# Hybrid decoder block with experts: the residual's gate moves from the weights to the product, and the row writes change buffer and queue

## The chip, the cores and the metric

One core of one Trainium2 chip runs the whole program. The metric is device time in microseconds (us) of one execution.

## The reference, cut to what matters

512 tokens of width 1024 go through one block: a modulated norm, a mixer (causal convolution and gated linear attention), a gated residual, a second norm with a router, and 32 experts of which each token uses two.

```
mod = c_act @ w_ada[l] + b_ada[l]
sh1, sc1, ga1, sh2, sc2, ga2 = jnp.split(mod, N_MOD, axis=-1)
u = modulate(rmsnorm(h, g_norm1[l]), sh1, sc1)
y = hybrid_mixer(...)                    # ends with: merged @ w_out
h = h + ga1[:, None, :] * y
u2 = modulate(rmsnorm(h, g_norm2[l]), sh2, sc2)
y2 = hierarchical_moe(u2, ...)           # 32 experts: (silu(t@w1)*(t@w3))@w2
h = h + ga2[:, None, :] * y2
```

`ga1` has one value per output column, so `ga1 * (merged @ w_out)` can be had by scaling the columns of `w_out` or by scaling the product.

## The kernel before

**Engines and queues.** TensorE (PE) works in the order of the program text. VectorE (DVE), ScalarE (ACT) and GpSimd (POOL) get an order from a planner that goes by estimated times, except where a stretch is marked as ordered by hand. SyncE (SP) issues nearly all loads, strictly in the order of the text: a transfer whose buffer or data is not ready holds up everything behind it. A transfer can also be issued from ACT's instruction stream; it then stands in ACT's order.

**Mixer.** Each weight piece is loaded, cast by ACT into a high part (`hi`), and the rest (`lo`) is taken by DVE or POOL in turn (`low_part`, line 384); PE multiplies three passes of high and low parts (line 393). The last part of the mixer is eight tiles of `w_gla_o` (`fmgo`, from `rawgo`, `higo`, `logo`). Beside it run the sums over `w_ada` for the second norm, the gates and the final norm (`acc_...`).

**Output projection.** `load_wo(c, k4)` brings `w_out` for column half `c` into `wo0` and `wo1` (two buffers each): load `woraw`, multiply by the gate row `ga1r` on DVE, cast on ACT, rest on POOL or DVE. Half 0 is loaded during the mixer from ACT's queue, half 1 later from SP. Half 0 is multiplied for all four token tiles first; then the list `ORDER` sets by hand what PE, DVE and ACT do. A step is a letter, a token tile t and a half or a depth index: W is three passes of half 1 for one of eight k, E the residual (`hx` += product), T four transposes of `hx` and ACT's copy of them, L and F the router's logits, Q squares, N the norm's root, R the choice of experts, P the positions, S `split_row`, G the first gather of tokens by matmuls with a selection (`gxf`).

**split_row(t)** scales row tile t twice on ACT for each half, into `mhi` and into `scaled`; POOL takes `mlo` from both; then the 128 finished rows go from `scaled` to the DRAM tensor `rowsd`, from where later gathers fetch tokens. `scaled` has two buffers in one allocation. `ga1r` and `scaled` use one slot of the pool in turn (tag "rows"), which the experts' input `xt` takes next.

**Experts.** Weights come in half slabs of 1 MB. `half_slab` hands out 14 slabs, then the two buffers each of `wo0` and `wo1`, in a fixed ring. Thirteen half slabs are issued before the output projection ends. The next five need the buffers of `wo0` and `wo1` and the slab `spare` (which holds the router's weights), and stand on SP behind the four `rowsd` writes. All later ones need a slab that the experts' own matmuls set free. `layer` (L1352: `hag`, `hbg`) multiplies with w1 and w3, `outputs` (L1382: `pog`) with w2, in groups of two pairs of experts.

Of the kernel before, what the change touches and what calls it, by code (L numbers as in the profile page):

```python
# [14 lines left out]
ALU = mybir.AluOpType  # L15
PSUM = bass.MemoryType.PSUM

P = 128
S = 512
D = 1024  # L20
ND = D // P
# [39 lines left out]
def kernel(ctx: ExitStack, tc: tile.TileContext, a, dbg=None):  # L61
    nc = tc.nc
    V, A, G, T, SY = nc.vector, nc.scalar, nc.gpsimd, nc.tensor, nc.sync

    def tt(out, in0, in1, op):
        return V.tensor_tensor(out, in0, in1, op=op)  # L66
# [27 lines left out]
    def tl(tag, name, shape=None, dt=F32):  # L94
        n, w = LOW.get(tag) or HIGH[tag]
        return (plo if tag in LOW else pa).tile([P, w] if shape is None else list(shape), dt, tag=tag, bufs=n, name=name)
# [285 lines left out]
    def low_part(lo, raw, hi):  # L382
        turn[0] += 1
        (V if turn[0] % LO_EVERY < lo_v[0] else G).tensor_tensor(lo, raw, hi.bitcast(F32), op=ALU.subtract)  # L384
# [135 lines left out]
    for t in range(NT):  # L520
        pz = bank("g", f"pz{t}")
        us = slice(t * P, (t + 1) * P)
# [220 lines left out]
    def big(tag, name, shape, dt=F32):  # L743
        return pr.tile(list(shape), dt, tag=tag, bufs=SLOTS[tag], name=name)
# [3 lines left out]
    def late(tag, name, n=1, shape=(P, 512), dt=F32):  # L748
        return plate[0].tile(list(shape), dt, tag=tag, bufs=n, name=name)

    ga1r = big("rows", "ga1r", (P, D))

    w_o = a["w_out"][0].rearrange("(k p) f -> p k f", p=P)
    wo = {}
# [1 line left out]
    def load_wo(c, k4):  # L756
        if c:
            rows = pslab.tile([P, 4, 512], F32, tag="slab", bufs=NW, name=f"woraw{k4}")
            SY.dma_start(rows, w_o[:, 4 * k4:4 * k4 + 4, 512:D])
        for i in range(2):  # L760
            k = 4 * k4 + 2 * i
            if c:
                raw = rows[:, 2 * i:2 * i + 2]
            else:
                raw = tl("raw", f"woraw{c}{k}", (P, 2, 512))
                A.dma_start(raw, w_o[:, k:k + 2, 0:512])

            tt(raw, raw, ga1r[:, c * 512:(c + 1) * 512].unsqueeze(1).to_broadcast([P, 2, 512]), ALU.mult)
            w = big(f"wo{i}", f"wo{c}{k4}{i}", (P, 2, 2, 512), F32R)
            A.copy(w[:, 0], raw)  # L770
            low_part(w[:, 1], raw, w[:, 0])
            for e in range(2):
                wo[c, k + e] = w[:, 0, e], w[:, 1, e]
# [77 lines left out]
    background += ada_col([(bfc, cols5[:, 0:8], None, PLAIN)], 0, "bf", w_af)  # L851
    background += ada_col([(afc, cols5[:, 8:16], cols5[:, 16:24], PLAIN)], D, "af", w_af)
    background += [lambda k4=k4: load_wo(0, k4) for k4 in range(2)]


# [65 lines left out]
    rowsd = pd.tile([S, D], F32, name="rowsd")  # L921
# [67 lines left out]
    for k4 in range(2):  # L989
        load_wo(1, k4)  # L990
# [31 lines left out]
    half_logits, banks, outs = {}, {}, {}  # L1022
# [28 lines left out]

    def residual(t, c):
        cs = slice(c * 512, (c + 1) * 512)
        tt(hx[:, t, cs], hx[:, t, cs], outs[t, c], ALU.add)

    def squares(t, c):
# [50 lines left out]
    def split_row(t):  # L1107

        us = slice(t * P, (t + 1) * P)
        for c in range(2):  # L1110
            row = hx[:, t, c * 512:(c + 1) * 512].rearrange("p (i k) -> p k i", k=ND)
            half = slice(us.start + c * 64, us.start + c * 64 + 64)
            hi = mhi[:, :, half]
            A.activation(hi, row, AF.Copy, scale=r2[:, t:t + 1])
            lo = mlo[:, :, half]
            u = scaled[:, t % 2, :, c * 64:c * 64 + 64]
            A.activation(u, row, AF.Copy, scale=r2[:, t:t + 1])
            G.tensor_tensor(lo, u, hi.bitcast(F32), op=ALU.subtract)
        SY.dma_start(rowsd[us], scaled[:, t % 2].rearrange("p k i -> p (k i)"))

    def token_weights(t, last):

# [44 lines left out]
    def gather_first(t, kk):  # L1167
        if t == 0:
            gathered.append(bank("mm" if kk else "bg", f"gxf{kk}"))
        gather(gathered[kk], kk, t, sel0)  # L1170

    STEPS = {"W": part, "T": turned, "L": logits_half, "F": logits, "N": rms, "R": route, "P": positions,
             "S": split_row, "G": gather_first, "E": residual, "Q": squares}

    ORDER = """E00 E10 E20 E30 T00 W00 W01 T10 L00 W02 W03 T20 L10 W04 W05 Q00 T30 L20 W06 W07 Q10 L30 Q20 Q30
               E01 W10 W11 T01 Q01 W12 L01 N0 S0 W13 F0 R0 W14 W15 W16 W17
               E11 W20 W21 T11 P0 Q11 W22 L11 N1 S1 W23 F1 R1 W24 W25 W26 W27
               E21 W30 W31 T21 P1 Q21 W32 L21 N2 S2 W33 F2 R2 W34 W35 W36 W37
               E31 P2 G00 G01 T31 Q31 G02 G03 L31 N3 G10 S3 F3 G11 R3 G12 G13 G20 G21 P3 G22 G23 G30 G31 G32 G33"""
    scaled = big("rows", "scaled", (P, 2, ND, P))  # L1180
    V.memset(lgs, -BIG)
    iota0 = late("iota0", "iota0", 1, (P, NE), U32)
    V.tensor_scalar(iota0, slotno[:, 0:NE], -1.0, None, op0=ALU.add)
# [8 lines left out]
    with tc.manual_schedule(engines={mybir.EngineType.PE, mybir.EngineType.DVE, mybir.EngineType.Activation}):  # L1192
        for step in ORDER.split():
            STEPS[step[0]](*map(int, step[1:]))
# [107 lines left out]
    def experts(n, cols, wts, name, early=False, tail=False):  # L1302
# [113 lines left out]
        def ending(behind):  # L1416
# [11 lines left out]
            def join(x, t):  # L1428
                combine([1], *sums[x], t)
                norm(t, "ABC".index(x), *sums[x], V if (x, t) in (('A', 3), ('C', 1), ('C', 3)) else G)  # L1430
# [3 lines left out]
            STEPS.update({x: lambda t, x=x: join(x, t) for x in sums})  # L1434
            ORDER = """M00 H00 L00 M01 H01 L01 M02 H02 J00 J01 L02 J02 J03 M03 H03 L03 J10 J11 J12 J13 X
                       M10 H10 L10 M11 H11 L11 M12 H12 M13 L12 H13 A0 A1 L13 M14 H14 A2 A3 L14 M15 H15
                       B0 B1 L15 B2 B3 S1 C0 R0 C1 R1 W0 C2 R2 W1 C3 R3 W2 W3"""
            with tc.manual_schedule(engines={mybir.EngineType.DVE, mybir.EngineType.Activation}):
                for step in ORDER.split():
                    STEPS[step[0]](*map(int, step[1:]))  # L1440
# [87 lines left out]
```

## Time and profile before

| | |
|---|---|
| median of 3 runs | 1016.86 us (1016.12 to 1017.1) |
| the profiled execution's own time | 1016.93 us |
| its span, first to last instruction | 1015.2 us |
| mean granted TensorE clock | 0.985 |
| busy: PE, DVE, ACT, POOL | 943.9, 555.7, 341.5, 184.0 us |
| moved by DMA | 283.96 MB |

Busy time is an average over stages with different limits: a busy PE can be a PE that is fed just in time, and an engine with a low share can hold up all others for some microseconds. The stages have to be read one by one, by windows and by who waited for whom.

### The profile page before, as it was taken

How to read it: one execution, taken by the hardware profiler on the slowest of the kernel's cores; microseconds unless marked ns; L12 is line 12 of the kernel's file. 1: busy time of each engine (PE TensorE's matmuls, PEld its weight loads, DVE VectorE, ACT ScalarE, POOL GpSimd, SP SyncE). 2: the span in 40 equal slices, each digit the busy share in tenths (PEclk: the TensorE clock that was granted, in tenths of full speed). 3: DMA queues.
4: the chain of work that ended last, by engine and by line, in shares of the span. 5: the costliest groups of instructions: out<-in, count | busy, mean ns of one | idle time of the engine just before them, and what ended most of it. 6: DMA issues, size and time to landing. Idle time of an engine off the chain costs nothing. (4 is left out here: it accounts for less than half of the span.)

```text
span 1015.2 us, 13708 instructions
## 1 busy us (share of the span) xinstructions
PE 943.9 (93%) x5250; PEld 609.8 (60%) x5250; DVE 555.7 (55%) x1041; ACT 341.5 (34%) x694; POOL 184.0 (18%) x122
## 2 busy tenths in 40 slices
PE   7999999999899999899999998989999898999993
PEld 4778899888678887687753353533435343343442
DVE  6778899889875898964541232331322233121346
ACT  7657323474135554342861102011110201002214
POOL 5513434323231212311210000000000000000005
PEclk9999999999999999999999999999999999999997
DMA  9863233215843677639569999999999999999972
GB/s 283 234 162 84 84 91 98 84 45 185 268 148 82 210 231 265 207 105 416 233 264 422 421 421 422 420 421 421 419 423 420 421 421 420 421 419 422 363 232 86
DMA packets 122409, 283.96 MB, mean 280 GB/s; under 512 B 10819, under 2 KB 87339, under 8 KB 99044
## 3 DMA queue, kind: packets, MB, share of 16 engines
q1 hardware_dynamic: 112700, 252.21, 65.9%
q10 hardware_dynamic: 7624, 27.27, 7.8%
q0 software_dynamic: 2016, 3.56, 0.9%
q8 instruction: 43, 0.70, 0.3%
q14 instruction: 26, 0.21, 0.1%
HBM read 282.61 MB, written 4.19 MB: 282 GB/s over the span
## 5 line engine op out<-in xcount | busy, mean ns | idle before, releaser
L384 POOL TENSOR_TENSOR low<-raww,hiw 128x1024 fp32r<-128x1024 f32 x36 | 91.7, 2546 | 211.1 <-ACT hiw L410 210.2
L1382 PE MATMUL pog<-p_w,htg 128*64 128x512 f32 x448 | 107.5, 602 | 5.0 <-DMA p_w<-in_w 5.0
L1387 ACT CAST ohlg<-pog 128x512 fp32r<-128x512 f32 (+2 forms) x38 | 19.7, 518 | 259.7 <-DVE pog L69 259.7
L66 DVE TENSOR_TENSOR s1g<-s1g,hbg 128x512 f32<-128x512 f32 (+1 forms) x18 | 11.1, 628 | 167.0 <-PE hbg L1352 167.0
L69 DVE SCALAR_TENSOR_TENSOR conv<-z,cols,conv 128x511 f32<-128x511 f32 (+14 forms) x120 | 88.7, 739 | 5.5 <-ACT conv L482 1.8
L393 PE MATMUL fmw<-uhi,low 128*128 128x512 f32 x224 | 91.4, 408 | 0.0
L393 PE MATMUL fmw<-uhi,hiw 128*128 128x512 f32 x224 | 90.2, 403 | 0.7 <-ACT sg L490 0.3
L393 PE MATMUL fmw<-ulo,hiw 128*128 128x512 f32 x224 | 90.5, 404 | 0.0
L66 DVE TENSOR_TENSOR hx<-hx,pcg 128x512 f32<-128x512 f32 (+1 forms) x76 | 49.2, 658 | 66.5 <-PE pcg L1407 66.5
L1382 PEld LDWEIGHTS pog<-p_w,htg 128*64 128x64 f32 x448 | 34.0, 138 | 76.1 <-issue 63.5
L393 PE MATMUL tm<-low,uhi 128*128 128x256 f32 x256 | 72.2, 284 | 0.0
L393 PE MATMUL tm<-hiw,uhi 128*128 128x256 f32 x256 | 71.9, 285 | 0.0
L393 PE MATMUL tm<-hiw,ulo 128*128 128x256 f32 x256 | 71.6, 281 | 0.0
L410 ACT CAST hiw<-raww 128x1024 fp32r<-128x1024 f32 x44 | 46.0, 1046 | 75.9 <-issue 43.0
L69 DVE SCALAR_TENSOR_TENSOR pog<-pog,wslg,ga2r 128x512 f32<-128x512 f32 (+2 forms) x38 | 25.6, 674 | 78.2 <-PE pog L1382 78.2
L393 PEld LDWEIGHTS fmw<-uhi,hiw 128*128 128x128 f32 x224 | 42.7, 191 | 10.5 <-ACT sg L490 0.8
L393 PEld LDWEIGHTS fmw<-ulo,hiw 128*128 128x128 f32 x224 | 42.7, 191 | 10.0
L393 PEld LDWEIGHTS tm<-low,uhi 128*128 128x128 f32 x256 | 48.1, 188 | 0.9 <-issue 0.5
L393 PEld LDWEIGHTS fmw<-uhi,low 128*128 128x128 f32 x224 | 42.6, 190 | 9.8 <-DVE low L384 0.2
L393 PEld LDWEIGHTS tm<-hiw,uhi 128*128 128x128 f32 x256 | 47.7, 188 | 0.8 <-issue 0.5
L393 PEld LDWEIGHTS tm<-hiw,ulo 128*128 128x128 f32 x256 | 48.1, 188 | 0.1
L1358 ACT ACTIVATE s1g<-hag 128x512 f32<-128x512 f32 x16 | 9.6, 598 | 103.4 <-PE hag L1352 103.4
(476 smaller groups left out, 1878.6 us busy)
## 6 DMA issues: line engine op xcount, KB each, us to landing
p_w<-in_w SPq DMA_DIRECT2D x182, 1024.0 KB, 19.8
raww<-in_w_in SPq DMA_DIRECT2D x44, 512.0 KB, 4.0
adaw<-in_w_ada SPq DMA_DIRECT2D x32, 256.0 KB, 5.6
aw_ga<-in_w_ada ACTq DMA_DIRECT2D x8, 1024.0 KB, 5.3
p_w2part<-in_w SPq DMA_DIRECT2D x12, 512.0 KB, 15.6
aw_a<-in_w_ada ACTq DMA_DIRECT2D x4, 1024.0 KB, 7.2
aw_b<-in_w_ada ACTq DMA_DIRECT2D x4, 1024.0 KB, 5.1
aw_bf<-in_w_ada_f ACTq DMA_DIRECT2D x4, 1024.0 KB, 5.5
```

The lines of the kernel that those rows point to most:

```text
L66: return V.tensor_tensor(out, in0, in1, op=op)
L69: return V.scalar_tensor_tensor(out, in0, scalar, in1, op0=op0, op1=op1)
L384: (V if turn[0] % LO_EVERY < lo_v[0] else G).tensor_tensor(lo, raw, hi.bitcast(F32), op=ALU.subtract)
L393: ins = T.matmul(*args, **kw)
L410: copy = A.copy(hi, raw)
L1358: return A.activation(s1s[q], ov, AF.Silu)
L1382: T.matmul(o[64 * e:64 * e + 64, :], ht[:, f, 64 * e:64 * e + 64], w["w2", e, c][:, f, :] if tail else w["w2", e, f // 2][:, f % 2, c0:c1] ...
L1387: A.copy(ohl[:, 0, c0:c1], prods[c])
```

## The change

The multiplication of `w_out` by `ga1r` in `load_wo` goes (eight instructions). `residual` gets a multiplication of the product, in PSUM, by `ga1r` (also eight). `ga1r` therefore lives until the last residual, and one allocation of two rows' size, `gate_rows`, holds it and one `scaled` buffer where there were two. The write of the normalised rows is issued from ACT's queue, not SP's. In `ORDER`, PE does one W more ahead of the transposes of the second halves, and one more around those of the first.

```diff
-    ga1r = big("rows", "ga1r", (P, D))
+
+    gate_rows = big("rows", "gate_rows", (P, 2, D))
+    ga1r, scaled = gate_rows[:, 0], gate_rows[:, 1].rearrange("p (k i) -> p k i", k=ND)
...
                 raw = tl("raw", f"woraw{c}{k}", (P, 2, 512))
                 A.dma_start(raw, w_o[:, k:k + 2, 0:512])
-
-            tt(raw, raw, ga1r[:, c * 512:(c + 1) * 512].unsqueeze(1).to_broadcast([P, 2, 512]), ALU.mult)
             w = big(f"wo{i}", f"wo{c}{k4}{i}", (P, 2, 2, 512), F32R)
...
     def residual(t, c):
         cs = slice(c * 512, (c + 1) * 512)
+        tt(outs[t, c], outs[t, c], ga1r[:, cs], ALU.mult)
         tt(hx[:, t, cs], hx[:, t, cs], outs[t, c], ALU.add)
...
-            u = scaled[:, t % 2, :, c * 64:c * 64 + 64]
+            u = scaled[:, :, c * 64:c * 64 + 64]
...
-        SY.dma_start(rowsd[us], scaled[:, t % 2].rearrange("p k i -> p (k i)"))
+
+        A.dma_start(rowsd[us], gate_rows[:, 1])
...
-    ORDER = """E00 E10 E20 E30 T00 W00 W01 T10 L00 W02 W03 T20 L10 W04 W05 Q00 T30 L20 W06 W07 Q10 L30 Q20 Q30
-               E01 W10 W11 T01 Q01 W12 L01 N0 S0 W13 F0 R0 W14 W15 W16 W17
-               E11 W20 W21 T11 P0 Q11 W22 L11 N1 S1 W23 F1 R1 W24 W25 W26 W27
-               E21 W30 W31 T21 P1 Q21 W32 L21 N2 S2 W33 F2 R2 W34 W35 W36 W37
-               E31 P2 G00 G01 T31 Q31 G02 G03 L31 N3 G10 S3 F3 G11 R3 G12 G13 G20 G21 P3 G22 G23 G30 G31 G32 G33"""
-    scaled = big("rows", "scaled", (P, 2, ND, P))
+    ORDER = """E00 E10 E20 E30 W00 T00 W01 W02 T10 L00 W03 W04 T20 L10 W05 W06 Q00 T30 L20 W07 Q10 L30 Q20 Q30
+               E01 W10 W11 W12 T01 Q01 W13 L01 N0 S0 W14 F0 R0 W15 W16 W17
+               E11 W20 W21 W22 T11 P0 Q11 W23 L11 N1 S1 W24 F1 R1 W25 W26 W27
+               E21 W30 W31 W32 T21 P1 Q21 W33 L21 N2 S2 W34 F2 R2 W35 W36 W37
+               E31 P2 G00 G01 G02 T31 Q31 G03 L31 N3 G10 S3 F3 G11 R3 G12 G13 G20 G21 P3 G22 G23 G30 G31 G32 G33"""
```

## Rows read from the trace of the kernel before

**Rows 1.** The page's 40 slices: TensorE busy tenths, and GB/s moved.

```profile
PE   7999999999899999899999998989999898999993
...
GB/s 283 234 162 84 84 91 98 84 45 185 268 148 82 210 231 265 207 105 416 233 264 422 421 421 422 420 421 421 419 423 420 421 421 420 421 419 422 363 232 86
```

**Rows 2.** Timeline of TensorE: starts of `hag`; start us, us, what, [idle before <-releaser].

```profile
565.02 1.51 PE L1352 MATMUL hag<-p_w,xtg__5324 128*64 128x512 f32 x6
...
622.68 1.51 PE L1352 MATMUL hag<-p_w,xtg__5630 128*64 128x512 f32 x6
...
921.87 3.65 PE L1352 MATMUL hag<-p_w,xtg__7162 128*64 128x512 f32 x16
```

**Rows 3.** Waits of TensorE, 740 to 1016: us in total, times, longest.

```profile
PE pog L1382 <- DMA p_w<-in_w: 5.0, 6, 1.4
```

**Rows 4.** Windows: busy us of PE, PEld, DVE, ACT, POOL; granted clock, DMA share, GB/s.

```profile
410.00:430.00 20.00, 15.11 (x62) 11.98 (x61) 19.52 (x17) 7.32 (x14) 5.37 (x3) 0.91 0.73 233
...
502.00:510.00 8.00, 8.00 (x58) 6.55 (x56) 5.37 (x23) 7.31 (x13) 2.71 (x3) 1.00 0.16 66
...
517.00:520.00 3.00, 1.98 (x9) 1.98 (x10) 0.00 (x0) 0.00 (x0) 0.96 (x1) 0.60 0.84 270
520.00:524.00 4.00, 4.00 (x22) 2.15 (x23) 2.24 (x7) 3.97 (x11) 0.00 (x0) 0.87 1.01 393
```

**Rows 5.** Timeline of SP, 490 to 526.

```profile
494.77 22.20 SPq L1119 DMA_DIRECT2D rowsd<-scaled  x4
517.06 3.03 SPq L947 DMA_DIRECT2D p_w<-in_w  x5
...
525.00 0.80 SPq L947 DMA_DIRECT2D p_w<-in_w  x2
```

**Rows 6.** Waits of TensorE, 330 to 520.

```profile
PE fmgo L393 <- DVE logo L384: 4.9, 1, 4.9
...
PE fmgo L393 <- DVE olo L69: 0.7, 1, 0.7
```

**Rows 7.** Tile `woraw`: duration ns min/median/max, first and last start.

```profile
L66 DVE TENSOR_TENSOR woraw<-woraw,ga1r x8: 1215/1220/3092, 402.3 to 459.8; 128x1024 f32<-128x1024 f32 x8
```

**Rows 8.** Timelines of VectorE and GpSimd, 416 to 422.

```profile
417.30 3.09 DVE L66 TENSOR_TENSOR woraw<-woraw,ga1r 128x1024 f32<-128x1024 f32 x1 [0.48 <-DMA woraw<-in_w_out]
...
420.91 1.21 DVE L384 TENSOR_TENSOR logo<-rawgo,higo 128x1024 fp32r<-128x1024 f32 x1
...
416.89 2.42 POOL L384 TENSOR_TENSOR wo<-woraw,wo 128x1024 fp32r<-128x1024 f32 x1 [6.50 <-ACT wo L770]
```

**Rows 9.** Timeline of VectorE: two instructions that depend on each other.

```profile
453.45 0.69 DVE L69 SCALAR_TENSOR_TENSOR th<-th,fmgo 128x512 f32<-128x512 f32 x1 [2.58 <-PE fmgo L393]
454.18 0.69 DVE L66 TENSOR_TENSOR yc<-yc,th 128x512 f32<-128x512 f32 x1
```

**Rows 10.** Timeline of ScalarE: its own transfers at 407, and the last token tiles.

```profile
407.61 4.88 ACTq L766 DMA_DIRECT2D woraw<-in_w_out  x2
...
509.74 0.61 ACT L1030 COPY spare<-pu 128x512 f32<-128x512 f32 x1
...
513.00 1.31 ACT L1117 ACTIVATE scaled<-hx,r 128x512 f32<-128x512 f32 x1
```

**Rows 11.** Timeline of TensorE, 500 to 528.

```profile
500.34 0.40 PE L262 MATMUL wo<-wo,mhi 128*128 128x512 f32 x1
...
501.04 0.40 PE L262 MATMUL wo<-wo,mhi 128*128 128x512 f32 x1
...
518.02 0.58 PE L1162 MATMUL gxf<-sel,mlo 128*128 128x256 f32 x1 [1.29 <-POOL mlo L1118]
...
521.32 7.09 PE L1352 MATMUL hag<-p_w,xtg__5005 128*64 128x512 f32 x32
```

**Rows 12.** DMA issues: KB each, median us from issue to landing.

```profile
p_w<-in_w SPq DMA_DIRECT2D x182, 1024.0 KB, 19.8
...
rowsd<-scaled SPq DMA_DIRECT2D x4, 512.0 KB, 3.0
```

## The prediction, written before the result

> **What bounds the kernel now.** I read the page's slices first. From the 22nd to the 37th of them (533 to 939 us) the chip moves 419 to 423 GB/s without a break, and TensorE is busy too [rows 1]. That is the experts' stage, and the question is which of the two sets its pace. The starts of the first matmuls of each group tell it. From group 1 to group 2 TensorE takes 622.68 - 565.02 = 57.66 us, but six groups to 921.87 take 356.85 us, 10.9 more than six times 57.66 [rows 2]. Groups of one shape that get slower while the stream stays flat are waiting for weights, and TensorE's list of waits names them in the later half of the stage [rows 3]. So at the end of the stage the stream of weights is the bound. What counts is when that stream begins to flow without gaps; TensorE alone could give back some 11 us before it became the bound itself.
>
> Then I looked for where the stream begins. From 502 to 510 us only 66 GB/s move; at 517 to 520 the rate is 270, then 393 [rows 4]. SP's timeline says why. From 494.77 to 516.97 it is busy with the four row writes, each of which waits for ACT, and at 517.06 five weight loads go out at once, with no wait between them: their buffers were all free by then [rows 5]. The next load goes out at 525.00, 3.68 us after the first expert matmul at 521.32, because that matmul's slab is the next buffer [rows 5, 11].
>
> Last, the mixer. TensorE is kept busy there except for one hole of 4.9 us that ends with `logo` from VectorE, and a small one of 0.7 [rows 6].
>
> **The change part by part.** I count each part by what it does to the start of the stream; after that every microsecond goes to the end one for one.
>
> *The weights' multiplications.* Eight go, of 1.22 us each except one of 3.09 [rows 7]. The four of half 1, the last of which starts at 459.8, I cost at nothing: they lie beside TensorE's products of half 0, which have yet to set free the buffers that the casts write; were that cover gone, they would cost at most 4 x 1.22 us. The four of half 0 lie in the mixer, where VectorE is busy 19.52 of 20 us [rows 4], and one of them is the hole: it waited for its load until 417.30, then took 3.09 us, beside a subtraction on GpSimd from 416.89 to 419.31, and `logo`, two places behind it, began at 420.91 [rows 8]. Without it `logo` can follow as soon as GpSimd is done, 419.3; TensorE then starts about 1.6 us sooner. If GpSimd's work also moves up, because its cast no longer waits for VectorE, up to the whole 4.9 comes back. The hole of 0.7 goes too: an `olo` stood behind another such multiplication [rows 6]. After the hole the granted clock of that window is 0.91 [rows 4], which costs 20 x 0.09 = 1.8 us at most, some of it in idle time, so 1.5. Upper bound 4.9 + 0.7 + 1.5 = 7.1 gained. Lower bound: the planner draws up a new order, and the next longest kind of hole is 1.3 us [rows 11], so 1.3 lost. I take 3.5 gained: nearly 3 of the 4.9, the 0.7, and nothing of the clock. All that follows, the first weight loads included, starts from the end of the mixer and moves with it.
>
> *The row writes leave SP.* The five loads no longer stand behind the rows. Their buffers come free when TensorE's W steps of the last token tile are done, the fifth when the router's last logits are taken, all before 517. In the kernel before, the five are 5.24 MB; of what moved from 517 on, 0.81 + 1.57 MB were through by 524, 0.52 of it a row tile [rows 4, 12], so 3.4 MB were left, which at 422 GB/s [rows 1] takes 8.0 us: the backlog ended at 532.0. In the changed kernel the five land in the idle stretch, and the stream then stands until a slab comes free, 3.68 us after the first expert matmul, plus some 1.7 us before bytes flow (3.0 us for a row tile less 1.24 for its bytes [rows 12]). With the first matmul at 521.32 that is 526.7, so the stream begins 5.3 us sooner. The move is worth 5.3 us less whatever the first expert matmul is delayed; the rest of the 15 us that SP saves is lost again, since no buffer is free.
>
> *The delay of the first expert matmul.* It hangs on the last `split_row`: `mlo` of tile 3 ends TensorE's wait at 518.02 [rows 11]. Four things lengthen the way there.
> (1) One more W ahead of T01 delays tile 0's copy by three passes, 0.7 us (501.04 - 500.34 from one W's start to the next [rows 11]).
> (2) Each residual is two instructions that depend on each other; such a pair starts 0.73 apart [rows 9]. For tile 0 the W hides it. For tile 1 it adds to (1), because its residual stands on VectorE behind tile 0's routing, which waits for ACT: 0.7 more.
> (3) From tile 2 on ACT is the tight engine: 7.31 of 8 us busy [rows 4], and the copy for tile 3 starts at 509.74, right behind tile 2's last scaling [rows 10]. A transfer takes 0.40 us to issue (two in 0.80 on SP [rows 5]) and now takes it from ACT. Tiles 1 and 2 together give 0.8, while W steps hide the residuals' extra time.
> Together 2.2 us, the lower bound.
> (4) With one buffer, the scaling of tile t+1 waits until tile t's rows are read out. Tile 2's rows go out at about 509.8 + 1.8 = 511.6 (1.8 is the sum so far less tile 2's own issue), and tile 3's first scaling into the buffer, at 513.00 before [rows 10], would start at 515.2. A row tile takes 3.0 us alone [rows 12]; then nothing waits. But now weights flow beside it. The nearest row is ACT's own 512 KB load beside SP's: the second of the two, which ends at 407.61 + 4.88 and so was issued at 412.1, ended VectorE's wait at 417.30, 5.2 us later [rows 8, 10]. Then tile 3 waits 1.6, and tile 2 in the same way at most as long. Queued on such a wait are all of ACT's later steps, its copies for TensorE among them, and on those TensorE's logits. I take 1.6 and 0.4, 2.0 of at most 3.2.
> Delay: 2.2 + 2.0 = 4.2 us, bounds 2.2 and 5.4.
>
> *Hidden.* The residuals of half 0 need 1.4 us each on VectorE (0.73 + 0.69 [rows 9]), where TensorE delivers one each 0.7; the W steps ahead of their transposes cover it. If not, T30 would be late by at most 4 x 0.7 us.
>
> *Sum.* 1016.93 - 3.5 - 5.3 + 4.2 = 1012.3 us, on the profiled execution's own time, which is 0.07 from the median of the runs.
>
> **Rivals.**
> *The stream gains nothing.* If the five buffers are in fact held until the last rows are out (a release that waits for the whole step), the five loads go out where they did. The empty stretch from 502 to 510 does not decide this, since SP was blocked; that the five went out without a wait at 517 speaks for buffers free earlier, not how much earlier. The rows move all the same, and the time is 1016.93 - 3.5 + 2.2 to 4.2, 1015.6 to 1017.6, in the middle 1016.6. Chance 0.12. A rule points to the same end: the Trainium skill, "DMA: Bandwidth & Descriptors", section "Issuing engines are not separate DMA queues", says that issuing from several engines saves only the sequencer's time to issue, usually small beside the transfer; that would make the move worth 1.6 us (four issues of 0.40) in place of my 5.3. The trace agrees only in part: of SP's 22.20 us at the row writes nearly all is waiting for ACT, not issuing [rows 5].
> *The mixer's hole stays.* VectorE has other work of a like size to put in its place, and the load of `woraw` still ends at 417.3, now in front of ACT's cast and the casts behind it. Then 1016.93 - 5.3 + 4.2 = 1015.8. Chance 0.15.
> *The hole closes wholly and the buffer never waits.* 1016.93 - 7.1 - 5.3 + 2.2 = 1006.7. Chance 0.08.
> *Slower: the single buffer.* Row writes on their own queue could crawl beside a full stream, as a 1 MB load takes 19.8 us in a full queue [rows 12]. Tile 2's rows would then be out at 531.4, tile 3 would wait 16.2 us, and the time would be 1016.93 - 3.5 - 5.3 + 2.2 + 16.2 = 1026.5. It decides for slower once the delay passes 10.8 us, that is once that row write takes over 12 us. ACT's loads beside SP's at 5.2 us speak against it, and only some three weight loads are in flight then. Chance 0.06, and 0.04 more for a new order of the planner that opens a larger hole than the old.
>
> **How the numbers follow.** A measurement of this kernel can tell about 0.2%, 2.0 us, from no change: faster is below 1014.8, slower above 1018.9. The forecast itself has 0.55 and a range of its own of 1009.0 (mixer 5.0, delay 2.4) to 1014.8 (mixer 2.0, delay 5.2). Faster: 0.55 + 0.08 and 0.03 of the cases just beyond, 0.66. Same: 0.12 + 0.15 less those 0.03, 0.24. Slower: 0.10. The range that leaves out 2 in 10 or less reaches from near the best case, 1007.0, to the upper end of the first rival, 1017.5.
>
> **What would show it.** In the changed kernel's profile: SP's loads 14 to 18 go out between about 500 and 515, one by one as W steps end, and SP then waits for `hag`; the next load goes out 3.7 us after the first `hag`. TensorE's waits before 460 lose the 4.9, and the output projection starts about 3.5 sooner. ACT shows waits for a transfer before `scaled` of tile 3, and the first `hag` stands at 521.32 - 3.5 + 4.2 = 522.0. The later groups' waits for `p_w` shrink by some 5 us in all. Wrong would be: a hole of like size elsewhere in the mixer; the five loads after the last row; ACT waiting over 5 us for a row write; or TensorE out of waits for weights, which would make its own pace the bound.

## The result, and the profile after

The changed kernel takes 1022.78 us in the median of 7 runs (1019.14 to 1025.93); the kernel before took 1017.1 beside it (1016.12 to 1020.43). The ratio is 1.0052, 95% interval 1.0032 to 1.0071: slower by about 5 us, where I had forecast 1012.3 and faster. The profiled execution of the changed kernel took 1025.93 us, the longest of the seven, with a span of 1024.2, so its own distance to the profile before, 9.0 us, is more than the change costs on the median.

What I said of SP's queue came true. SP's timeline of the changed kernel, in three stretches (506 to 507, 511 to 520, 520 to 541): the five loads go out in the idle stretch, one by one as their buffers come free, and not at 517 in one go as in [rows 5].

```profile
506.69 0.33 SPq L947 DMA_DIRECT2D p_w<-in_w  x1
...
512.11 7.52 SPq L947 DMA_DIRECT2D p_w<-in_w  x4
...
539.80 0.80 SPq L947 DMA_DIRECT2D p_w<-in_w  x2
```

But the next load, which must wait for the first `hag`, goes out at 539.80 and not at 525.00. ACT's timeline, 506 to 536, shows who is late:

```profile
507.62 0.35 ACTq L1121 DMA_DIRECT2D rowsd<-gate_rows  x1
...
513.80 1.33 ACT L1118 ACTIVATE gate_rows<-hx,r 128x512 f32<-128x512 f32 x1 [1.73 <-DMA rowsd<-gate_rows]
...
517.47 0.33 ACTq L1121 DMA_DIRECT2D rowsd<-gate_rows  x1
...
527.14 1.21 ACT L1118 ACTIVATE gate_rows<-hx,r 128x512 f32<-128x512 f32 x1 [5.93 <-DMA rowsd<-gate_rows]
...
530.63 0.33 ACTq L1121 DMA_DIRECT2D rowsd<-gate_rows  x1
...
533.35 1.11 ACT L1326 ACTIVATE xtg__5004<-gxf,b2x,a2x 128x256 f32<-128x256 f32 x2 [2.16 <-DMA rowsd<-gate_rows]
```

The times in brackets are ACT's idle time and what ended it. The write of tile 1 goes out at 507.62 and holds the buffer until about 513.7, 6.1 us; that of tile 2 goes out at 517.47 and holds it until about 527.1, 9.6 us. The last one, with no load beside it, needs some 2.6 and still keeps ACT waiting 2.16 before the experts' input `xtg`, which takes the same slot. TensorE's list of waits, 330 to 560 (total, times, longest), has the wait that the late rows cause in its first line. The other lines shown are the mixer's hole, the wait for GpSimd's part of the last tile, and a new hole in the mixer:

```profile
PE gxf L1164 <- ACT mhi L1115: 4.1, 1, 4.1
PE fmgo L393 <- DVE logo L384: 2.7, 1, 2.7
...
PE gxf L1164 <- POOL mlo L1119: 2.1, 1, 2.1
PE pr_ga L835 <- ACT ga2r L838: 1.4, 1, 1.4
```

The mixer's hole of 4.9 [rows 6] has become 2.7, and the new one of 1.4 stands before it. The windows of the changed kernel (columns as in [rows 4]) show the last part of the output projection with TensorE half empty, and the chip moving little from 530 on:

```profile
410.00:430.00 20.00, 15.91 (x58) 12.19 (x57) 19.96 (x17) 7.63 (x10) 8.64 (x3) 0.85 0.80 251
...
510.00:520.00 10.00, 7.56 (x56) 6.40 (x54) 5.70 (x22) 7.19 (x13) 2.55 (x2) 0.99 0.94 333
520.00:530.00 10.00, 5.78 (x36) 5.33 (x36) 2.83 (x16) 4.07 (x4) 1.27 (x1) 0.84 0.64 243
530.00:540.00 10.00, 8.01 (x33) 4.79 (x35) 4.22 (x27) 6.76 (x20) 1.26 (x1) 0.66 0.13 53
```

TensorE's timeline ends that stretch; the first `hag` [rows 11] is 14.2 us later than before. The gathers `gxf` run right up to it, so ACT's 2.16 before `xtg` costs TensorE nothing here:

```profile
529.53 0.39 PE L1164 MATMUL gxf<-sel,mhi 128*128 128x256 f32 x1 [4.14 <-ACT mhi L1115]
531.99 0.58 PE L1164 MATMUL gxf<-sel,mlo 128*128 128x256 f32 x1 [2.08 <-POOL mlo L1119]
...
535.49 7.72 PE L1353 MATMUL hag<-p_w,xtg__5004 128*64 128x512 f32 x32
```

### The profile page after: what moved, and what is told of

Read it like the earlier page. It is cut to its first block, busy times and chain, and to the rows that moved or that the text cites. A ratio compares the mean times of both kernels' runs of the same rounds, so it can differ in the third digit from the quotient of the medians.

```text
span 1024.2 us, 13702 instructions
## 1 busy us (share of the span) xinstructions
PE 948.2 (93%) x5250; PEld 612.2 (60%) x5250; DVE 550.2 (54%) x1041; ACT 342.9 (33%) x694; POOL 182.8 (18%) x122
## 5 line engine op out<-in xcount | busy, mean ns | idle before, releaser
L1383 PE MATMUL pog<-p_w,htg 128*64 128x512 f32 x448 | 102.6, 601 | 2.8 <-DMA p_w<-in_w 2.8
L393 PEld LDWEIGHTS fmw<-uhi,hiw 128*128 128x128 f32 x224 | 42.7, 191 | 10.8 <-ACT hiw L410 0.8
```

Of the source, the lines that this page charges most:

```text
L393: ins = T.matmul(*args, **kw)
L1383: T.matmul(o[64 * e:64 * e + 64, :], ht[:, f, 64 * e:64 * e + 64], w["w2", e, c][:, f, :] if tail else w["w2", e, f // 2][:, f % 2, c0:c1] ...
```

## The experiments

For each profile I take two numbers: the distance from the first addition into `hx` to the first `hag` (the chain; 48.26 before, from 473.06 to 521.32), and the point from which the weights flow without a gap. That point is the first load behind the five plus 1.7 us or, where the five go out together after the last row, their first issue plus 14.9 us (517.06 to 532.0, as the prediction counted it).

**Theory 1**: a row write that is issued while weight loads are under way is served late, and with one buffer ACT waits for it. **Theory 2**: the loss comes from the mixer. **Theory 3**: one buffer is too few by itself; **3b**: ACT's queue is slow by itself.

**e1: a second buffer.** The changed kernel, with the odd tiles in a buffer `odd` of its own (three buffers of `lh`, the logits' halves, make room for it).

```diff
-            u = scaled[:, :, c * 64:c * 64 + 64]
+            u = (scaled, odd)[t % 2][:, :, c * 64:c * 64 + 64]
...
-        A.dma_start(rowsd[us], gate_rows[:, 1])
+        A.dma_start(rowsd[us], (scaled, odd)[t % 2].rearrange("p k i -> p (k i)"))
...
+    odd = late("odd", "odd", 1, (P, ND, P))
```

> The changed kernel with a second buffer for the scaled rows (tiles 1 and 3 use it; to make room the logits' halves get 5 buffers in place of 8). Theory 1, the row write: ScalarE waits for single row writes that stand behind weight loads (in the changed kernel 3 us at tile 2 and 7 us at tile 3), and this sets the loss. Then these waits are gone, from E00 to the first hag it takes about 51 us in place of 58.3, and the time falls by about 7, to 1015 to 1016. Theory 2, the mixer: the loss is the 4.1 us by which the output projection starts later, and the waits at the rows are paid for by the earlier loads; then the waits go but the time stays within 2 of the changed kernel's, about 1022.

1013.13 us (10 runs; before 1017.76), ratio 0.9951 (0.9933 to 0.9969). That is below the forecast of 1015 to 1016. The chain is 50.40, and SP's timeline, 501 to 515 and 520 to 530, has the loads early again and the next one at 527.90:

```profile
502.40 11.80 SPq L947 DMA_DIRECT2D p_w<-in_w  x5
...
527.90 0.80 SPq L947 DMA_DIRECT2D p_w<-in_w  x2
```

One buffer more turns the change from slower to faster.

**e2: rows on SP, one buffer. e3: the five loads held back until the last row.** e2 is the changed kernel with the row writes issued by SP. e3 leaves them on ACT's queue, but SP issues the last 16 rows of the last tile, so that the loads behind it wait.

```diff
-        A.dma_start(rowsd[us], gate_rows[:, 1])
+        SY.dma_start(rowsd[us], gate_rows[:, 1])          # e2
...
+        A.dma_start(rowsd[t * P:(t + 1) * P - 16], gate_rows[0:P - 16, 1])          # e3, last tile
+        SY.dma_start(rowsd[(t + 1) * P - 16:(t + 1) * P], gate_rows[P - 16:P, 1])
```

> The changed kernel with the row writes issued from SP again, the single buffer kept. The five weight loads stand behind the last row again, so nothing flows beside the rows. Theory 1: each row is out in 3 us, ScalarE waits under 1 us for a buffer, from E00 to the first hag 50 to 51 us; the early loads are lost, so the time is that of before plus 2 to 3 and plus what the mixer does (0 to 4): 1019 to 1023. Theory 3, that one buffer is too few whatever flows beside: the waits of some 3 and 7 us stay, and with the early loads lost as well the time goes to about 1028.

> The changed kernel, but the last 16 rows of the last tile go from SP, so that SP holds the five weight loads back until the last row is ready; the other rows stay on ScalarE's queue. Theory 1: with no loads beside, a row write on ScalarE's queue takes 3 to 3.5 us and nothing waits over 1 us; time as with the rows on SP, 1019 to 1023. Theory 3b, that ScalarE's queue is slow by itself: row writes still take 6 to 10 us, and the time is 1026 or more.

e2: 1020.6, ratio 1.0029 (1.0012 to 1.0045). e3: 1020.39, ratio 1.0031 (1.0018 to 1.0044). The chains are 50.52 and 50.36. ACT's timeline of e3 has the one buffer, ACT's queue, and no wait at a scaling:

```profile
502.73 0.35 ACTq L1122 DMA_DIRECT2D rowsd<-gate_rows  x1
507.06 1.30 ACT L1118 ACTIVATE gate_rows<-hx,r 128x512 f32<-128x512 f32 x1
...
510.72 0.33 ACTq L1122 DMA_DIRECT2D rowsd<-gate_rows  x1
515.18 1.31 ACT L1118 ACTIVATE gate_rows<-hx,r 128x512 f32<-128x512 f32 x1
```

So neither the one buffer nor ACT's queue costs the chain anything by itself: theories 3 and 3b fall. The wait needs loads beside the rows. ACT does wait 3.0 us (e2) and 3.4 us (e3) for the last row before the experts' input, more than either expectation allows, but the chains show that TensorE's first `hag` is no later for it.

**e4: the gate alone.** The gate on the product and the new written order, two buffers, rows on SP: the kernel of e1 with one line more.

```diff
-        A.dma_start(rowsd[us], (scaled, odd)[t % 2].rearrange("p k i -> p (k i)"))
+        SY.dma_start(rowsd[us], (scaled, odd)[t % 2].rearrange("p k i -> p (k i)"))
```

> Gate on the product and the new order alone: two row buffers, rows from SP as before (logits' halves in 5 buffers). Theory 1: the gate costs the 2.2 us of the longer chain at most, less what the mixer gains: from E00 to the first hag 50 to 51 us, time 1016 to 1020. Theory 2: the mixer's part is the loss, E00 starts at 477 again and the time is 1021 or more.

1020.43, ratio 1.0025 (1.001 to 1.0041), chain 50.43. The time is just above theory 1's 1016 to 1020, but theory 2 falls: the additions start at 474.56, not at 477. The gate's part costs some 2.5 us (1.0 to 4.2 by the interval) and gives nothing; e1, which differs only in the rows' queue, is 7.3 lower in the median and 5.4 in the profiled executions.

**e5: the queue alone. e6: queue and buffer, without the gate.** Both are the kernel before with `A.dma_start` at the row write; e6 has one `scaled` in place of two.

```diff
-        SY.dma_start(rowsd[us], scaled[:, t % 2].rearrange("p k i -> p (k i)"))
+        A.dma_start(rowsd[us], scaled[:, t % 2].rearrange("p k i -> p (k i)"))          # e5
+        A.dma_start(rowsd[us], scaled.rearrange("p k i -> p (k i)"))                    # e6
```

> The kernel before with one edit: the row writes go out from ACT's queue; two buffers stay, the gate stays on the weights. Theory 1 (the row write is slow because it stands behind weight loads that were issued just before it, and this costs only where the one buffer makes ACT wait for it): rows 1 and 2 land 5 to 10 us after their issue, as in the changed kernel, but nobody waits for them; the first expert matmul comes 0 to 1.2 us later than before (up to three issues of 0.40 on ACT), the stream starts 5 to 6 us sooner, the time is 1012 to 1013, 4 to 5 below the kernel before. Theory 3b (ACT's queue is slow by itself and holds up ACT): the first expert matmul over 3 us later and the time 1015 or more. The gate's price goes by the difference to the two-buffer form of the change (1013.1): if the gate's move to the product costs 2.2 in the chain and gives nothing in the mixer, this kernel is 1 to 2 us below that.

> The kernel before with two edits: rows from ACT's queue and one buffer for them; the gate stays on the weights, the written order is the old one. Theory 1: ACT waits for the landing of row tiles 1 and 2, some 2 and 6 us, the first expert matmul comes 8 to 10 us later than before, less than the 57.55 - 48.26 = 9.3 of the changed kernel by at most the gate's 2.2; the stream's sooner start of 5 to 6 is more than lost; 1019 to 1022. Rival (the loss comes from the gate on the product and the new order, and the waits of ACT only show it): the first expert matmul within 2 us of the one before and the time 1012 to 1014.

e6: 1020.41, ratio 1.0038 (1.0026 to 1.0051), chain 57.61: the changed kernel's loss without its gate, and the rival falls. e5 missed: 1016.95, ratio 1.0001 (0.9988 to 1.0015), chain 52.12, neither theory 1's number nor 3b's. ACT's timeline of e5 has the reason:

```profile
516.19 0.33 ACTq L1119 DMA_DIRECT2D rowsd<-scaled  x1
...
523.70 1.93 ACT L1325 ACTIVATE xtg__5005<-gxf,b2x,a2x 128x256 f32<-128x256 f32 x4 [6.96 <-DMA rowsd<-scaled]
```

There are two buffers for the scaling, but both lie in the slot that `xtg` takes next. The last write goes out at 516.19 beside the loads and holds that slot for some 7.4 us. TensorE stands before its first `hag` for 4.7 us, starts it at a granted clock of 0.68 (520 to 530), and the next load goes out 6.7 us behind the first `hag` in place of 3.7. Theory 1 had to be made wider: whoever needs the buffer next pays, the next scaling or the experts' input. In e1 the last tile lies in `odd`, so that `xtg` does not wait for it.

**e7: the loads between the rows, on one queue.** The kernel before, rows on SP, with a step X in `ORDER` that issues the next of the five loads.

```diff
-                E21 W30 W31 T21 P1 Q21 W32 L21 N2 S2 W33 F2 R2 W34 W35 W36 W37
-                E31 P2 G00 G01 T31 Q31 G02 G03 L31 N3 G10 S3 F3 G11
+                E21 W30 W31 X T21 P1 Q21 W32 L21 N2 S2 W33 F2 R2 W34 W35 X X W36 W37 X
+                E31 P2 G00 G01 T31 Q31 G02 G03 L31 N3 G10 S3 X F3 G11
```

> The kernel before with its row writes on SP, two buffers and the gate on the weights; only the order in which SP issues is new: the five weight loads that stood behind the four row writes go out between them, one after the second W of the last token tile, two after its sixth, one after its eighth, one after the last logits. If the blocked queue is the whole of the gain (theory 1), the loads land in the idle stretch, no instruction is added to ACT, the first expert matmul stays within 1 us of 48.3 after the first residual, and the stream starts 5 us sooner: 1011 to 1013. If it needs two queues (a row write must wait on a queue of its own), the loads still go out late behind the waiting rows and the time is 1015 to 1017.

1016.67, ratio 0.9998 (0.9983 to 1.0012), chain 53.07: a miss, by the same wait. SP's timeline and ACT's of e7:

```profile
509.49 0.32 SPq L1119 DMA_DIRECT2D rowsd<-scaled  x1
509.90 1.76 SPq L947 DMA_DIRECT2D p_w<-in_w  x3
516.34 0.33 SPq L1119 DMA_DIRECT2D rowsd<-scaled  x1
```

```profile
525.21 1.93 ACT L1325 ACTIVATE xtg__5015<-gxf,b2x,a2x 128x256 f32<-128x256 f32 x4 [8.83 <-DMA rowsd<-scaled]
```

The loads are early on one queue as well. The last row write, behind three loads on the same queue, holds the slot for 8.8 us.

**e8: rows on GpSimd's queue, one buffer.** The changed kernel with one line more.

```diff
-        A.dma_start(rowsd[us], gate_rows[:, 1])
+        G.dma_start(rowsd[us], gate_rows[:, 1])
```

> The changed kernel, its one buffer kept, with the row writes issued from GpSimd's queue in place of ACT's. The five loads still go out early from SP. If what delays a row write is the order of issue that ACT's and SP's queues share, a third queue is served beside the loads: rows 1 and 2 land within 3 to 4.5 us, ACT does not wait, the first expert matmul comes 50 to 52 us after the first residual and the time is 1013 to 1016. If it is the loads' bytes in the DMA engines themselves, whichever queue: rows 1 and 2 take 6 and 9 us again, the first expert matmul comes 57 us after the first residual and the time is 1021 to 1024.

1022.22, ratio 1.005 (1.0033 to 1.0067), chain 57.67. ACT's timeline and GpSimd's:

```profile
509.37 1.33 ACT L1118 ACTIVATE gate_rows<-hx,r 128x512 f32<-128x512 f32 x1 [1.27 <-DMA rowsd<-gate_rows]
...
523.39 1.21 ACT L1118 ACTIVATE gate_rows<-hx,r 128x512 f32<-128x512 f32 x1 [7.08 <-DMA rowsd<-gate_rows]
```

```profile
506.17 0.59 POOL L1121 DMA_DIRECT2D rowsd<-gate_rows  x1
...
514.30 0.57 POOL L1121 DMA_DIRECT2D rowsd<-gate_rows  x1
```

The write of tile 2 takes 9.0 us on a third queue too; that of tile 1, which went out 3.3 us after the only load ahead of it, takes 3.1. A queue of its own does not protect a row write. The Trainium skill, "DMA: Bandwidth & Descriptors", section "Issuing engines are not separate DMA queues", says that transfers of the scalar, sync and GpSimd engines run on the same 16 DMA engines and interleave there. These three queues agree in that none of them spares the row write; how far the packets interleave, the last section shows.

**e9 and e10: the last tile out of the experts' slot.** e5 and e7, each with the odd tiles in `odd` as in e1, the gate on the weights.

```diff
-    scaled = big("rows", "scaled", (P, 2, ND, P))
+    scaled = big("rows", "scaled", (P, ND, P))
+    odd = late("odd", "odd", 1, (P, ND, P))
```

> The kernel before with two edits: rows from ACT's queue, and the second of the two row buffers lies in a place of its own, so that the slot which the experts' input takes next holds only the rows of tiles 0 and 2; the gate stays on the weights. Theory 1, wider (a late row write costs whoever needs its buffer next: the next scaling where there is one buffer, the experts' input where the last tile lies in its slot): the 7.0 us that ACT waited there for the last row write go, the first expert matmul comes 48.3 to 49.3 us after the first residual, the next load 3.8 behind it and the stream 1.7 behind that, at about 527.3 against 532.0, so 4 to 5 below the kernel before. Rival (ACT waits at the experts' input for something else, or two queues cost by themselves): it stays at 52 and the time at that of the kernel before.

> The same with the rows on SP and the five loads issued between them. Theory 1: as with ACT's queue, and without the issues on ACT: the first expert matmul 48.3 after the first residual, the time 4.5 to 5.5 below the kernel before. If SP must hold a queue free for a waiting row: the time of the kernel before.

e9: 1011.66 (5 runs; before 1017.13), ratio 0.9945 (0.9926 to 0.9964), chain 48.73. e10: 1011.35 (8 runs), ratio 0.9947 (0.9928 to 0.9965), chain 46.84. Both are as theory 1 has it or slightly better, and the best two of all. Moving the place of one buffer (with `lh` cut to five, as in e1) took 5.3 us off e5 and off e7. In e9 ACT still waits 2.67 us before the experts' input, now for tile 2's write, which lies in that slot; TensorE does not wait for it. SP's timeline of e10 and TensorE's:

```profile
510.40 0.32 SPq L1119 DMA_DIRECT2D rowsd<-scaled  x1
510.81 1.77 SPq L947 DMA_DIRECT2D p_w<-in_w  x3
517.27 0.33 SPq L1119 DMA_DIRECT2D rowsd<-odd  x1
517.69 7.64 SPq L947 DMA_DIRECT2D p_w<-in_w  x3
```

```profile
518.64 0.38 PE L1162 MATMUL gxf<-sel,mlo 128*128 128x256 f32 x1 [1.29 <-POOL mlo L1118]
...
520.40 0.27 PE L1162 MATMUL gxf<-sel,mlo 128*128 128x256 f32 x1
520.61 5.80 PE L1353 MATMUL hag<-p_w,xtg__5016 128*64 128x512 f32 x26
```

**e11 and e12: the gate's price, and the written order.** e11 is e1 again, beside e9; e12 is e1 with the old `ORDER`, of which this is one line.

```diff
-               E11 W20 W21 W22 T11 P0 Q11 W23 L11 N1 S1 W24 F1 R1 W25 W26 W27
+               E11 W20 W21 T11 P0 Q11 W22 L11 N1 S1 W23 F1 R1 W24 W25 W26 W27
```

> The changed kernel with a second row buffer in a place of its own, once more, beside the two kernels that differ from it in the gate. If the gate on the product costs 2.2 in the chain and gives nothing in the mixer, it is 1.5 to 2.5 slower than the rows from ACT's queue with the gate on the weights. If the mixer does gain the 3.5 that I forecast, it is 1 or more faster.

> The changed kernel with a second row buffer in a place of its own and the written order of before. The new order delays each tile's copy by one W, 0.7 us, but hides the second instruction of each residual behind it. If the W is the larger part (my term 1), the first expert matmul comes 49.7 after the first residual in place of 50.4 and the time is 0 to 0.7 lower; if the residual's pair stands open without it (term 2), TensorE's wait for hx grows from 1.1 to over 3 and the time is 0.5 to 2 higher.

e11: 1014.9 (12 runs), ratio 0.9974 (0.9962 to 0.9987), 3.2 slower than e9. e12: 1013.93 (12 runs), ratio 0.9969 (0.9954 to 0.9983), chain 49.36. By e11 and e12 the gate on the product costs 2 to 3 us, and the mixer gives nothing for it. The size is uncertain: e1, the same kernel as e11, stood at 0.9951, only 0.6 us above e9. The old order is not told apart from the new by time. TensorE's wait for `hx` in 475 to 545 stays at 1.1 in e12, so the residual's second instruction is hidden without the extra W too, and term 2 of my chain does not show.

## Why the prediction was wrong, point by point

**What bounds the kernel** held. In the thirteen profiles beside that of before, the point where the stream begins, from 6.0 us sooner to 9.5 later, and the end of the span move together within 1.0 us; six of them:

| kernel | stream begins, against 532.0 | span, against 1015.2 |
|---|---|---|
| after | 539.80 + 1.7 = 541.5: +9.5 | 1024.2: +9.0 |
| e4 | 520.61 + 14.9 = 535.5: +3.5 | 1018.0: +2.8 |
| e6 | 534.0 + 1.7 = 535.7: +3.7 | 1018.4: +3.2 |
| e5 | 531.0 + 1.7 = 532.7: +0.7 | 1014.9: -0.3 |
| e1 | 527.90 + 1.7 = 529.6: -2.4 | 1012.6: -2.6 |
| e10 | 524.3 + 1.7 = 526.0: -6.0 | 1008.7: -6.5 |

**The row writes leave SP, -5.3**: held. The stream begins 10.7 us after the first `hag` before, 6.0 in the changed kernel and 5.5 in e1: -4.7 and -5.2. The rival in which the five loads gain nothing falls, and with it the reading that another engine's queue saves only the time to issue: what it saved is the wait in front of the loads.

**The chain, +2.2**: held within the spread. From the first addition it is 50.36 to 50.52 in e1 to e4 against 48.26, and 49.5 and 49.4 in e11 and e12, so one profile is good to about 1 us. But that distance leaves out the first multiplication by `ga1r`, which now stands between the product and the addition. VectorE's timelines of the changed kernel and of the one before:

```profile
477.20 0.70 DVE L66 TENSOR_TENSOR wo<-wo,gate_rows 128x512 f32<-128x512 f32 x1 [0.81 <-PE wo L264]
477.94 0.69 DVE L66 TENSOR_TENSOR hx<-hx,wo 128x512 f32<-128x512 f32 x1
```

```profile
473.06 0.69 DVE L66 TENSOR_TENSOR hx<-hx,wo 128x512 f32<-128x512 f32 x1 [5.06 <-PE wo L264]
```

Counted from this multiplication, which starts when TensorE's product is done, it is 51.1 to 51.3 in e1 to e4, +2.9, and 50.2 and 50.1 in e11 and e12, +1.9. The prediction put the multiplications of half 0 at nothing (*Hidden*). The first of them puts the first addition 0.74 us later; whether all of that reaches `hag`, profiles that differ by 1 us do not decide.

**The mixer, -3.5**: wrong; the rival "the mixer's hole stays" was right here. From its first to its last matmul `fmgo` takes 57.1 to 58.9 us in the eight kernels with the gate on the product and 57.3 to 58.4 in the six with it on the weights. VectorE's timeline of the changed kernel shows what came in place of the slow multiplication ahead of `logo` [rows 8]:

```profile
414.65 2.92 DVE L791 TENSOR_SCALAR acc_af<-aw_af,cact 128x1024 f32<-128x1024 f32 x1
...
419.40 1.28 DVE L69 SCALAR_TENSOR_TENSOR acc_af<-aw_af,cact,acc_af 128x1024 f32<-128x1024 f32 x1
420.60 1.22 DVE L384 TENSOR_TENSOR wo<-woraw,wo 128x1024 fp32r<-128x1024 f32 x1
421.73 0.68 DVE L69 SCALAR_TENSOR_TENSOR th<-th,fmgo 128x512 f32<-128x512 f32 x1
422.33 1.28 DVE L69 SCALAR_TENSOR_TENSOR acc_af<-aw_af,cact,acc_af 128x1024 f32<-128x1024 f32 x1
423.52 1.22 DVE L384 TENSOR_TENSOR logo<-rawgo,higo 128x1024 fp32r<-128x1024 f32 x1
```

VectorE is busy 19.96 of the 20 us now and was 19.52: sums and a rest of `wo` moved up into the room, and `logo` stands behind them. In the changed kernel's own profile `fmgo` even takes 58.9 us against 57.3, at a granted clock of 0.85 in place of 0.91 from 410 to 430.

**The row writes' landing, step (4), +2.0**: this is the step that failed, and the one that makes the change slower. I took a row tile beside weights at 5.2 us, from ACT's loads in the mixer; measured are 6.1 and 9.6. Tile 3 waits 5.9 in place of 1.6 and tile 2 waits 1.7 in place of 0.4. Together they lengthen the chain from 50.4 to 57.55, 7.1 us in place of 2.0. ACT's wait before the experts' input, 2.2, I had not counted; it adds nothing in this kernel, but it is what took the gain from e5 and e7. The nearest row was the wrong one: ACT's load stood beside one load of SP's, the row tile behind three of 1 MB that had been let go early by this very change. So early loads and late rows are one effect, and I had sized them as two. The rival "slower: the single buffer" had the mechanism; its point of decision was a delay of 10.8, and with nothing from the mixer it decides at 7.3 (10.8 less 3.5), which 2.2 + 7.1 passes.

With the measured terms the sum is 1016.93 + 0 - 4.7 + 2.9 + 7.1 = 1022.2, and by the ratio (1.0052 of 1016.9) it is 1022.2. That they meet to the digit is luck: with the +1.9 of e11 and e12 the sum would be 1021.2. Of the 9.9 us by which the forecast of 1012.3 missed, 5.1 are step (4), 3.5 the mixer, and the rest the two other terms. In the profiled execution the first addition stands 4.9 us later, at 477.94 in place of 473.06. Of these, 2.4 are there when `fmgo` begins, at 398.5 in place of 396.1, ahead of the changed instructions; 1.6 are `fmgo`'s greater length and 0.7 the first multiplication. The other kernels with the gate on the product begin `fmgo` between 394.9 and 399.5, so the 2.4 are spread between executions and not the change.

## What to carry to other kernels

Before a queue is unblocked, look at what the freed transfers will run beside: here the loads that went out sooner made the row writes issued just behind them 3 to 8 us later, and a buffer with one owner less had to wait for it. Count for each written-out buffer who takes its place next, also the tile of a later stage that shares its slot; with the last tile in a place of its own the same move was worth 0.5%, from either queue. A busy engine that loses an instruction in front of a late result does not hand the result over sooner if its planner has other work for the gap.

## What the runs showed of the hardware that I had not expected

A 512 KB write with no load ahead of it took 2.6 to 3.1 us (e8's first, on GpSimd's queue, 4.2). It took 3.1 when one 1 MB load had gone out 3.3 us ahead, 6.1 when that was 0.9 us ahead (6.6 at 0.4 us, in e6), and 9.0 to 9.7 with three loads 4 to 6 us ahead, on ACT's queue and on GpSimd's, and 8.8 on SP's own. With three loads 1.6 to 3.5 us ahead it was 10.5 in e11 and 10.6 in e9. The three loads alone don't account for 9.6: 3.15 MB at 420 GB/s from 512.11 + 1.7 would be through at 521.3, and the row's own bytes 1.2 us later, while the buffer came free at 527.1. The packets of the changed kernel show the rest. The DMA queues from the issue of tile 2's row, 517.47, to 521.5, and from there to 527.1 (packets, MB, share of the 16 engines; q1 is SP's queue, q10 ACT's):

```profile
q1 hardware_dynamic: 184, 1.36, 99.2%
```

```profile
q1 hardware_dynamic: 207, 1.45, 62.2%
q10 hardware_dynamic: 144, 0.52, 23.3%
```

For the first 4.0 us nothing of the row moves. It begins when 2.70 of the three loads' 3.15 MB are through, and then runs beside the remaining 0.45 and some 1.0 MB of the fourth load, which was issued 1.8 us behind it. So the row waits out nearly all that was issued ahead of it on the other queue, and then shares with what came behind. In e8 it is the same on GpSimd's queue: issued at 514.30, its first packet starts at 518.2. The Trainium skill, "DMA: Bandwidth & Descriptors", section "Queues, rings and completion order", says that a DMA engine takes the queues it has work for in turn, packet by packet; an even share with SP's loads would let a 512 KB write through in about 2 x 1.24 + 1.7 = 4.2 us, an estimate from [rows 12]. The measured 9.6 does not agree, nor do the first 4.0 us without a packet of the row; why it gets no turn in them stays open.

In the kernel before, the last gathers before `hag` take 0.41 us each, after idle stretches of 0.69 and 1.29 us of TensorE; the granted clock is 0.60 on the mean of 517 to 520 [rows 4] and 0.50 from 519 to 521, which is the level of 1.2 GHz. In e10 they take 0.28, after idle stretches of 0.67 and 1.29, at a clock of 1.00, the level of 2.4 GHz. The windows of both (columns as in [rows 4]):

```profile
519.00:521.00 2.00, 2.00 (x12) 2.00 (x11) 0.40 (x1) 1.00 (x3) 0.00 (x0) 0.50 1.00 303
```

```profile
519.00:521.00 2.00, 2.00 (x17) 1.68 (x17) 1.05 (x3) 1.65 (x4) 0.00 (x0) 1.00 1.03 258
```

From the first of them to the first `hag` it is 3.30 us in the one and 1.97 in the other, nearly all of the 1.4 by which e10's chain, 46.84, is shorter than that of before. Why the clock fell in the one and not in the other stays open; in e9, with the same idle stretches (0.67 and 1.29), it fell as well.
